# Short f32 products in a recurrence: halves of the TensorE array by turns, and live blocks only

## The chip, the cores and the metric

The kernel runs on one core of one Trainium2 chip, as a single launch. The metric is device time in microseconds (us) of that launch.

## The reference

One step of a diffusion backbone with one trunk layer: a half-step feed-forward (FFN), a token mixer, a second half-step FFN, and a last RMSNorm. 128 context tokens and 1024 latent tokens go through the same weights; width 1024, all in f32. The mixer adds an attention branch and a bidirectional recurrence (HGRN2) of 8 heads with 64 key and 64 value channels. The change is in the recurrence:

```python
b = jnp.cumsum(logf.reshape(B, n, CHUNK, H, DK), axis=2)
diff = b[:, :, :, None] - b[:, :, None, :]
decay = jnp.where(mask, jnp.exp(jnp.where(mask, diff, 0.0)), 0.0)
A = jnp.einsum('bntshk,bnthk,bnshk->bnhts', decay, qc, kc)
o_intra = jnp.einsum('bnhts,bnshv->bnthv', A, vc)
...
def step(S, inp):
    gj, dSj = inp
    return jnp.exp(gj)[..., None] * S + dSj, S
...
o_inter = jnp.einsum('bnthk,bnhkv->bnthv', qc * jnp.exp(b), S_prev)
return (o_intra + o_inter).reshape(B, T, H, DV), s_final
```

For each head the state S decays channel by channel with the forget gate f and takes in the outer product of k = 1 - f and v; the output is S read by q. It is done once forwards and once backwards in time, and the two outputs are added.

## The kernel before

All activations lie transposed: channels on the 128 partitions, the 1152 tokens (1024 latent, 128 context) along the free axis, in three blocks of 384 (`CW`), visited in `ORDER` = 2, 0, 1. The order of phases is FFN 1, mixer (recurrence, then attention), merge and FFN 2. The large products are done on values split into a high and a low float32r part, three matmuls for one (`mm3`, L446 to L448, tiles `mm` in the recurrence). The recurrence's own products are plain f32.

The recurrence (`hgrn`) loops over 8 heads. Partitions 0 to 63 (`A`) hold the head's forward channels, 64 to 127 (`B`) the backward ones. A block of 384 tokens is three tiles of 128 tokens. For each head and block:

- `scan_pre` makes, within groups of 8 tokens, running products of gates (`X`, `Y`), from them decayed keys `Kb` and queries `Qb`, then `KE` and the block's part of `QP` (keys carried to the end of their group, queries from its start), and the group's whole decay `Tm`.
- `scan_lev` builds the 128 x 128 matrix of each tile. First the base products, `Kb` by `Qb` for `A` and for `B` apart (L858, each contracting 64 rows), masked into `A1` and `A2` within groups of 8. Then four decay levels m = 8, 16, 32, 64: `kr[m]` is a copy of `KE` in which only the half-groups that count are not zero, one matmul for a tile with the full 128 rows (L873) gives both directions, and `KE` and `QP` are multiplied by the decay of a neighbour half-group (L884). The outcome goes into `A1` through a mask (L888), at level 64 by two ScalarE copies (L890, L891). Then `Af = A1 + A2`, a transpose of `KE` (L899), and the state increment `dS` (L905).
- After the three blocks `scan_out` runs the states `S` over the eight latent tiles on VectorE (L916) and forms the outputs: for each block and tile a product of `V` with `Af` (L924) and, for latent tiles, of `S` with `QP` (L928), added in one PSUM tile `po`. A head's 64 value channels take one half of the array's columns, rows `r` of `po`; ScalarE copies them to `oT`.

These are generators: between their steps the loop in `hgrn` takes one turn of projection work of the next heads (`work`, 12 matmuls of `mm` in a turn) and one step of the next block's `scan_pre`, and this is the order in which instructions are written; the scheduler of the framework may move them. PSUM has three banks for level and base products (`lv`), three for transposes, increments and outputs (`sm`) and two for projections (`mm`). A PSUM tile is reused when the engine that reads it is done.

Of the kernel before, what the change touches and what calls it, by code (L numbers as in the profile page):

```python
# [9 lines left out]
F32 = mybir.dt.float32  # L10
F32R = mybir.dt.float32r
BF16 = mybir.dt.bfloat16
U8 = mybir.dt.uint8
# [6 lines left out]
P = 128  # L20
# [6 lines left out]
CW = 384  # L27
# [3 lines left out]
ORDER = (2, 0, 1)  # L31
# [56 lines left out]
class Trunk:  # L88
# [514 lines left out]

    def mixer_consts(self, cp):
        nc, a = self.nc, self.a
        self.mask = cp.tile([P, 5, P], U8, name="mask")
        mf = self.tt(F32, "maskf")[:, : 5 * P]
        nc.scalar.dma_start(mf, a["mask"])
        nc.vector.tensor_copy(self.mask.rearrange("p a b -> p (a b)"), mf)
        self.onesb = cp.tile([P, P], F32, name="onesb")  # L610
        nc.vector.memset(self.onesb, 0.0)
        nc.vector.memset(self.onesb[0:64, 0:64], 1.0 / 64)
        nc.vector.memset(self.onesb[64:128, 64:128], 1.0 / 64)
        self.onesq = cp.tile([P, P], F32, name="onesq")
        nc.vector.memset(self.onesq, 1.0 / 384)
        self.onesk = cp.tile([P, P], F32, name="onesk")
        nc.vector.memset(self.onesk, 1.0 / 256)
# [89 lines left out]
    def hgrn(self):  # L707
        nc = self.nc
        self.mmb = 2
        for tag, n in (("lv", 3), ("sm", 3), ("mm", 2)):  # L710
            self.pp.tile([P, 512], F32, tag=tag, bufs=n, name=tag)
        f32 = lambda n, sh: self.fp.tile(sh, F32, name=n)
        A, B = slice(0, 64), slice(64, P)
        self.kr = {m: [f32(f"kr{m}_{i}", [P, CW]) for i in range(1)] for m in (8, 16, 32, 64)}
        self.XY = [f32(n, [P, 48, 8]) for n in "XY"]
        self.A1 = [f32(f"A1_{i}", [P, 3, P]) for i in range(2)]
        self.A2 = [f32("A2", [P, 3, P])]
        for m in self.kr:
            for t in self.kr[m]:
                nc.vector.memset(t, 0.0)  # L720
        for t in self.XY:
            nc.vector.memset(t[:, :, 3:4], 1.0)
        for t in self.A1 + self.A2:
            nc.vector.memset(t, 0.0)
        self.cnt = 0
        heads = [{} for _ in range(H)]
        pairs = [{} for _ in range(4)]
        sgs = [self.proj_sg(j) for j in range(2 * KT)]

        def feed(h):  # L730
            p = h // 2
            r = [self.proj_f(5 * p + h % 2, h, heads[h])]
            if h % 2 == 0:
                r += [self.proj_q(5 * p + 2, pairs[p]), self.proj_v(5 * p + 3, pairs[p])]
            return r

        for i, _ in enumerate(weave(feed(0))):
            if i < 12:
                next(self.tail, None)
            if i == 11:  # L740
                assert next(self.tail, 1)
        def scan_of(h):
            p = h // 2
            if h % 2 == 0:
                pairs[p]["o"] = self.tt(F32, "oT")
            d = heads[h]
            d.update(pairs[p])
            d["h"], d["QP"], d["As"] = h, self.tt(F32, "QP"), {}
            d["Gall"] = self.fp.tile([P, 9], F32, tag="Gall", bufs=2, name="Gall")
            return d  # L750

        def work_of(h):
            p = h // 2
            work = feed(h + 1) if h + 1 < H else []
            if h and h % 2 == 0:
                work = [self.proj_gate(5 * p - 1, p - 1, pairs[p - 1]["o"])] + work
            while len(work) < 4:
                work.append(sgs.pop())
            return chain(*work)

        d = scan_of(0)
        for _ in self.scan_pre(d, ORDER[0]):
            pass
        for h in range(H):
            work = work_of(h)
            for n, b in enumerate(ORDER):
                nd, pre = None, iter(())
                if n < NCH - 1:
                    pre = self.scan_pre(d, ORDER[n + 1])
                elif h + 1 < H:  # L770
                    nd = scan_of(h + 1)
                    pre = self.scan_pre(nd, ORDER[0])
                for _ in self.scan_lev(d, b):
                    next(work, None)
                    next(pre, None)
                for _ in pre:
                    next(work, None)
            for _ in self.scan_out(d):
                next(work, None)
            for _ in work:  # L780
                pass
            oT, d = d["o"], nd
        for _ in self.proj_gate(19, 3, oT):
            pass
# [51 lines left out]
    def scan_lev(self, d, b):  # L836
        nc = self.nc
        V, QP, hh, Gall = d["V"], d["QP"], d["h"] % 2, d["Gall"]
        A, B = slice(0, 64), slice(64, P)
        c0 = b * CW  # L840
        tmp = self.tmp
        if b == ORDER[0]:
            d["dS"] = self.fp.tile([P, 9, 64], F32, tag="dS", bufs=1, name="dS")
            S = d["S"] = self.fp.tile([P, 8, 64], F32, tag="S", bufs=1, name="S")
# [3 lines left out]
        A1, A2 = self.A1[self.cnt % 2], self.A2[0]  # L848
        self.cnt += 1
        Kb, Qb, KE, Tm = d["pre"]  # L850
        bc = lambda t, m: t.unsqueeze(2).to_broadcast([t.shape[0], t.shape[1], m])
        qp = QP[:, c0 : c0 + CW]
        lv = lambda: self.pp.tile([P, 3, P], F32, tag="lv", bufs=3, name="lv")
        mb = lambda i: self.mask[:, i].unsqueeze(1).to_broadcast([P, 3, P])
        for r, dst, mi in ((A, A1, 0), (B, A2, 1)):
            ps = lv()
            for j in range(3):
                nc.tensor.matmul(ps[:, j], Kb[r, ts(j, P)], Qb[r, ts(j, P)], start=True, stop=True)  # L858
            nc.vector.copy_predicated(dst, mb(mi), ps)
        hm = lambda t, m: t.rearrange("p (n h m) -> p n h m", h=2, m=m)  # L860

# [5 lines left out]
        key_half(8)  # L867
        yield
        for li, m in enumerate((8, 16, 32, 64)):
            kr = self.kr[m][0]  # L870
            ps = lv()
            for j in range(3):
                nc.tensor.matmul(ps[:, j], kr[:, ts(j, P)], qp[:, ts(j, P)], start=True, stop=True)  # L873
            tv = Tm.rearrange("p (n h) -> p n h", h=2)
            tL, tR = tv[:, :, 0], tv[:, :, 1]
            Tn = Gall[:, 3 * b : 3 * b + 3] if m == 64 else tmp(f"T{2 * m}", 3, (P, CW // (2 * m)))
            for r, eng, t, side, tt in (
                (A, nc.vector, KE, 0, tR),
                (B, nc.vector, KE, 1, tL),
                (A, nc.gpsimd, qp, 1, tL),  # L880
                (B, nc.vector, qp, 0, tR),
            ):
                v = hm(t, m)[r, :, side]
                eng.tensor_tensor(v, v, bc(tt[r], m), ALU.mult)  # L884
            nc.vector.tensor_mul(Tn, tL, tR)
            if m < 64:
                key_half(2 * m)
                nc.vector.copy_predicated(A1, mb(2 + li), ps)  # L888
            else:
                nc.scalar.copy(A1[A, :, B], ps[A, :, B])  # L890
                nc.scalar.copy(A1[B, :, A], ps[B, :, A])  # L891
            Tm = Tn
            yield
        Af = tmp("Af", 4, (P, 3, P))
# [14 lines left out]
    def scan_out(self, d):  # L909
        nc = self.nc  # L910
        h, V, QP, Gall, S, dS = d["h"], d["V"], d["QP"], d["Gall"], d["S"], d["dS"]
        A, B = slice(0, 64), slice(64, P)
        nc.sync.dma_start(self.o["st"][h], dS[:, 8])
        for j in range(7):
            for r, s0, s1, g in ((A, j, j + 1, j), (B, 7 - j, 6 - j, 7 - j)):
                nc.vector.scalar_tensor_tensor(S[r, s1], S[r, s0], Gall[r, g : g + 1], dS[r, g], ALU.mult, ALU.add)  # L916
        yield
        off = 64 * (h % 2)
        r = slice(off, off + 64)
        for b in ORDER:  # L920
            po = self.pp.tile([P, 3, P], F32, tag="sm", bufs=3, name="po")
            for j in range(3):
                t = 3 * b + j
                nc.tensor.matmul(  # L924
                    po[r, j], V[:, t * P + off : t * P + off + 64], d["As"][b][:, j], start=True, stop=(t == 8)
                )
                if t < 8:
                    nc.tensor.matmul(po[r, j], S[:, t], QP[:, ts(t, P)], start=False, stop=True)  # L928
            nc.scalar.copy(d["o"][r, b * CW : (b + 1) * CW], po[r].rearrange("p a b -> p (a b)"))
            yield  # L930

    def rec_norm(self, c, oT, sq):
# [834 lines left out]
def mask_table():  # L1767
    import numpy as np

    s, t = np.arange(P)[:, None], np.arange(P)[None, :]  # L1770
    same = lambda b: s // b == t // b
    m = [same(8) & (s <= t), same(8) & (s >= t)]
    m += [same(2 * b) & ~same(b) for b in (8, 16, 32)]
    return np.concatenate(m, 1).astype(np.float32)


# [33 lines left out]
```

## Time and profile before

| | |
|---|---|
| median of 3 runs | 2985.35 us (2982.49 to 2985.77) |
| span of the profiled execution, first to last instruction | 2987.2 us |
| busy time in it: PE, VectorE (DVE), ScalarE (ACT), GpSimd (POOL) | 2879.0, 2026.6, 1238.5, 1029.7 us |
| mean granted TensorE clock | 0.987 |
| first and last base product (L858) | 885.7 and 1470.8 us |
| first and last head output product (L924) | 955.4 and 1500.0 us |

No time of the profiled execution beside its span was recorded. PE is TensorE's matmuls, PEld its weight loads, which overlap them. An f32 matmul leaves two records of weight load and matmul in the trace (a transpose one). The time of a PE record includes its way through the array, so records overlap; how fast PE goes is read from start to start. In lists of groups the columns are busy time, mean ns of one, and idle time of the engine just before with what ended it; in lists of waits, the total, the count and the longest one.

### The profile page before, as it was taken

How to read it: one execution, taken by the hardware profiler on the slowest of the kernel's cores; microseconds unless marked ns; L12 is line 12 of the kernel's file. 1: busy time of each engine (PE TensorE's matmuls, PEld its weight loads, DVE VectorE, ACT ScalarE, POOL GpSimd, SP SyncE). 2: the span in 40 equal slices, each digit the busy share in tenths (PEclk: the TensorE clock that was granted, in tenths of full speed). 3: DMA queues.
4: the chain of work that ended last, by engine and by line, in shares of the span. 5: the costliest groups of instructions: out<-in, count | busy, mean ns of one | idle time of the engine just before them, and what ended most of it. 6: DMA issues, size and time to landing. Idle time of an engine off the chain costs nothing. (4 is left out here: it accounts for less than half of the span.)

```text
span 2987.2 us, 49338 instructions
## 1 busy us (share of the span) xinstructions
PE 2879.0 (96%) x18498; PEld 2739.4 (92%) x18498; DVE 2026.6 (68%) x4238; ACT 1238.5 (41%) x2374; POOL 1029.7 (34%) x939
## 2 busy tenths in 40 slices
PE   6999999999989999999998999989999999999998
PEld 5999999999979989898997777779999999999997
DVE  7677777677677777878456677756674665546665
ACT  6432332321364555555244777731462233232112
POOL 0223223453243333323244445532342322226431
PEclk9999999999999999999998999999999999999999
DMA  6643433743121111111110000242352322235211
GB/s 242 205 142 120 133 121 118 265 138 116 63 64 56 38 44 38 54 38 51 60 48 12 16 15 25 62 161 82 123 176 94 106 88 75 74 110 210 91 45 64
DMA packets 151470, 282.37 MB, mean 95 GB/s; under 512 B 19200, under 2 KB 83648, under 8 KB 151232
## 3 DMA queue, kind: packets, MB, share of 16 engines
q1 hardware_dynamic: 151088, 278.90, 28.3%
q8 instruction: 146, 2.39, 0.3%
q14 instruction: 92, 0.75, 0.1%
q10 hardware_dynamic: 144, 0.33, 0.0%
HBM read 215.64 MB, written 63.52 MB: 93 GB/s over the span
## 5 line engine op out<-in xcount | busy, mean ns | idle before, releaser
L1560 PE MATMUL b<-xo,wo 128*128 128x288 f32 x3552 | 484.8, 296 | 0.0
L1560 PEld LDWEIGHTS b<-xo,wo 128*128 128x128 f32 x3552 | 476.6, 188 | 0.0
L475 DVE SCALAR_TENSOR_TENSOR x<-dn,modt,x 128x256 f32<-128x256 f32 (+4 forms) x728 | 353.4, 505 | 169.2 <-PE dn L448 168.1
L235 POOL TENSOR_TENSOR wl<-raw,wh 128x1024 fp32r<-128x1024 f32 (+1 forms) x106 | 235.4, 2222 | 418.7 <-ACT wh L234 353.0
L1560 PE MATMUL b<-bh,wo 128*128 128x288 f32 x1776 | 365.9, 295 | 0.8 <-ACT et L1570 0.8
L446 PE MATMUL mm<-xh,wh 128*128 128x384 f32 (+1 forms) x1008 | 360.5, 358 | 6.1 <-DVE q L665 4.1
L448 PE MATMUL mm<-xh,wl 128*128 128x384 f32 (+1 forms) x1008 | 342.2, 340 | 2.1 <-POOL wl L235 1.9
L447 PE MATMUL mm<-xl,wh 128*128 128x384 f32 (+1 forms) x1008 | 342.0, 339 | 0.0
L1560 PEld LDWEIGHTS b<-bh,wo 128*128 128x128 f32 x1776 | 289.1, 188 | 1.0 <-ACT et L1570 1.0
L1560 PE MATMUL b<-bl,wo 128*128 128x288 f32 x888 | 261.7, 295 | 0.0
L234 ACT CAST wh<-raw 128x1024 fp32r<-128x1024 f32 (+1 forms) x108 | 104.3, 968 | 257.2 <-PE dn L447 165.8
L1535 ACT CAST wo<-raw 128x512 fp32r<-128x512 f32 x185 | 114.7, 621 | 229.0 <-PE b L1560 116.9
L446 PEld LDWEIGHTS mm<-xh,wh 128*128 128x128 f32 (+1 forms) x1008 | 190.2, 189 | 16.0 <-DVE q L665 4.9
L446 PE MATMUL dn<-hh,wh 128*128 128x384 f32 (+2 forms) x576 | 196.3, 341 | 2.0 <-DVE x L475 1.1
L1536 DVE TENSOR_TENSOR wo<-raw,wo 128x512 fp32r<-128x512 f32 x185 | 127.1, 688 | 103.3 <-ACT wo L1535 100.3
L448 PE MATMUL dn<-hh,wl 128*128 128x384 f32 (+2 forms) x576 | 194.7, 338 | 1.0 <-POOL wl L235 1.0
L447 PE MATMUL dn<-hl,wh 128*128 128x384 f32 (+2 forms) x576 | 194.2, 337 | 0.0
L448 PEld LDWEIGHTS mm<-xh,wl 128*128 128x128 f32 (+1 forms) x1008 | 189.7, 188 | 3.6 <-POOL wl L235 2.2
L447 PEld LDWEIGHTS mm<-xl,wh 128*128 128x128 f32 (+1 forms) x1008 | 190.4, 189 | 1.7 <-issue 0.4
L1638 POOL TENSOR_TENSOR hl<-hr,hh 128x1152 fp32r<-128x1152 f32 x44 | 117.9, 2689 | 197.1 <-ACT hh L1637 105.8
L1292 POOL TENSOR_TENSOR ehl<-e,ehl 128x512 fp32r<-128x512 f32 x93 | 122.1, 1318 | 143.8 <-ACT ehl L1290 83.6
L306 DVE SCALAR_TENSOR_TENSOR junk<-wada,cb 128x512 bf16<-128x512 f32 x224 | 165.9, 741 | 5.3 <-DMA wada<-in_w_aT 4.5
(388 smaller groups left out, 7125.0 us busy)
## 6 DMA issues: line engine op xcount, KB each, us to landing
raw<-in_w SPq DMA_DIRECT2D x148, 256.0 KB, 2.9
raw<-in_w SPq DMA_DIRECT2D x58, 512.0 KB, 3.7
wada<-in_w_aT SPq DMA_DIRECT2D x112, 256.0 KB, 2.8
hr<-hs SPq DMA_DIRECT2D x44, 576.0 KB, 5.6
hs<-et SPq DMA_DIRECT2D x148, 144.0 KB, 1.8
raw<-in_w_in SPq DMA_DIRECT2D x41, 512.0 KB, 3.6
hb<-hd SPq DMA_DIRECT2D x44, 288.0 KB, 3.2
x<-in_xT SPq DMA_DIRECT2D x16, 576.0 KB, 6.2
```

Of the source, the lines that this page charges most:

```text
L234: pin(self.nc.scalar.copy(wh, raw))
L235: pin((eng or self.nc.gpsimd).tensor_sub(wl, raw, wh))
L306: nc.vector.scalar_tensor_tensor(junk, ws[n % 2], 1.0, cs[s], ALU.mult, ALU.mult, accum_out=o)
L446: pin(nc.tensor.matmul(ps, wh, xh, start=start and i == 0, stop=False))
L447: pin(nc.tensor.matmul(ps, wh, xl, start=False, stop=False))
L448: pin(nc.tensor.matmul(ps, wl, xh, start=False, stop=stop and i == n - 1))
L475: nc.vector.scalar_tensor_tensor(self.x[m][:, a:b], ps[:, a - lo : b - lo], self.modt[:, gm, m, s : s + 1], self.x[m][:, a:b], ALU.mult, A ...
L1292: eng.tensor_sub(el, e, eh)
L1535: nc.scalar.copy(wh, src[i])
L1536: nc.vector.tensor_sub(wl, src[i], wh)
L1560: nc.tensor.matmul(ps, w[:, k], x[:, k, :QW], start=first, stop=last, skip_group_check=home != i)
L1638: nc.gpsimd.tensor_sub(hl, raw, hh)
```

## The change

Three edits in the recurrence:

1. Base products: the matmuls of the row halves `A` and `B` are written by turns, tile by tile, and both masked copies come after them.
2. Levels 32 and 64: instead of one matmul of a tile with 128 rows and masked result, only the blocks that count are formed. At level 32 there are four for a tile, each with 64 rows, 32 columns of keys and 32 of queries; at level 64 two, of 64 by 64. Forward blocks go into one `lv` bank and backward ones into another. ScalarE copies each kind of block into `A1` (four copies at level 32, two at level 64). Level 64 reads `KE` itself; `kr[64]`, its copies and the mask of level 32 are gone.
3. Head outputs: instead of three groups by block, two groups by distance from the middle of the sequence, tiles (3,4), (2,5) and then (1,6), (0,7), (8). The first of each pair goes to PSUM rows and array columns 0 to 63, the second to 64 to 127. Each group's two halves are copied out apart.

```diff
@@ scan_lev
-        for r, dst, mi in ((A, A1, 0), (B, A2, 1)):
-            ps = lv()
-            for j in range(3):
+        pair = (A, lv()), (B, lv())
+        for j in range(3):
+            for r, ps in pair:
                 nc.tensor.matmul(ps[:, j], Kb[r, ts(j, P)], Qb[r, ts(j, P)], start=True, stop=True)
+        for dst, mi, (_, ps) in zip((A1, A2), (0, 1), pair):
             nc.vector.copy_predicated(dst, mb(mi), ps)
...
         for li, m in enumerate((8, 16, 32, 64)):
-            kr = self.kr[m][0]
-            ps = lv()
-            for j in range(3):
-                nc.tensor.matmul(ps[:, j], kr[:, ts(j, P)], qp[:, ts(j, P)], start=True, stop=True)
+            blocks = []
+            if m < 32:
+                kr, ps = self.kr[m][0], lv()
+                for j in range(3):
+                    nc.tensor.matmul(ps[:, j], kr[:, ts(j, P)], qp[:, ts(j, P)], start=True, stop=True)
+            else:
+                kr, pair = KE if m == 64 else self.kr[m][0], (lv(), lv())
+                blocks = [
+                    (ps, r, slice(k, k + m), slice(q, q + m))
+                    for u in range(0, P, 2 * m)
+                    for ps, r, k, q in ((pair[0], A, u, u + m), (pair[1], B, u + m, u))
+                ]
+                for j in range(3):
+                    kj, qj = kr[:, ts(j, P)], qp[:, ts(j, P)]
+                    for ps, r, k, q in blocks:
+                        nc.tensor.matmul(ps[k, j, :m], kj[r, k], qj[r, q], start=True, stop=True)
...
-            if m < 64:
+            if m < 32:
                 key_half(2 * m)
                 nc.vector.copy_predicated(A1, mb(2 + li), ps)
-            else:
-                nc.scalar.copy(A1[A, :, B], ps[A, :, B])
-                nc.scalar.copy(A1[B, :, A], ps[B, :, A])
+            for ps, _, k, q in blocks:
+                nc.scalar.copy(A1[k, :, q], ps[k, :, :m])
@@ scan_out
-        for b in ORDER:
+        for pairs, lows, highs in (((3, 4), (2, 5)), (2, 4), (4, 6)), (((1, 6), (0, 7), (8,)), (0, 2), (6, 9)):
             po = self.pp.tile([P, 3, P], F32, tag="sm", bufs=3, name="po")
-            for j in range(3):
-                t = 3 * b + j
-                nc.tensor.matmul(
-                    po[r, j], V[:, t * P + off : t * P + off + 64], d["As"][b][:, j], start=True, stop=(t == 8)
-                )
-                if t < 8:
-                    nc.tensor.matmul(po[r, j], S[:, t], QP[:, ts(t, P)], start=False, stop=True)
-            nc.scalar.copy(d["o"][r, b * CW : (b + 1) * CW], po[r].rearrange("p a b -> p (a b)"))
+            at = lambda t: po[A, t - lows[0]] if t < lows[1] else po[B, t - highs[0]]
+            for pair in pairs:
+                for t in pair:
+                    w = V[:, t * P + off : t * P + off + 64]
+                    nc.tensor.matmul(at(t), w, d["As"][t // 3][:, t % 3], start=True, stop=(t == 8))
+                for t in pair:
+                    if t < 8:
+                        nc.tensor.matmul(at(t), S[:, t], QP[:, ts(t, P)], start=False, stop=True)
+            for half, (t0, t1) in ((A, lows), (B, highs)):
+                pv = po[half, : t1 - t0].rearrange("p a b -> p (a b)")
+                nc.scalar.copy(d["o"][r, t0 * P : t1 * P], pv)
             yield
```

The mask table and its tile shrink from five masks to four, and the `kr[64]` buffer goes.

More of the change, by code (lines that the diff above doesn't have):

```diff
@@ L605, in mixer_consts @@
         nc, a = self.nc, self.a
-        self.mask = cp.tile([P, 5, P], U8, name="mask")
-        mf = self.tt(F32, "maskf")[:, : 5 * P]
+        self.mask = cp.tile([P, 4, P], U8, name="mask")
+        mf = self.tt(F32, "maskf")[:, : 4 * P]
         nc.scalar.dma_start(mf, a["mask"])
@@ L713, in hgrn @@
         A, B = slice(0, 64), slice(64, P)
-        self.kr = {m: [f32(f"kr{m}_{i}", [P, CW]) for i in range(1)] for m in (8, 16, 32, 64)}
+        self.kr = {m: [f32(f"kr{m}_{i}", [P, CW]) for i in range(1)] for m in (8, 16, 32)}
         self.XY = [f32(n, [P, 48, 8]) for n in "XY"]
@@ L1772, in mask_table @@
     m = [same(8) & (s <= t), same(8) & (s >= t)]
-    m += [same(2 * b) & ~same(b) for b in (8, 16, 32)]
+    m += [same(2 * b) & ~same(b) for b in (8, 16)]
     return np.concatenate(m, 1).astype(np.float32)
```

## The prediction

> **What bounds the kernel now.** I read the page's first part, then the busy times of the recurrence stage (880 to 1520 us, found by the lines of the changed tiles), then the waits inside it.
>
> ```profile
> span 2987.2 us, 49338 instructions
> PE 2879.0 (96%) x18498; PEld 2739.4 (92%) x18498; DVE 2026.6 (68%) x4238; ACT 1238.5 (41%) x2374; POOL 1029.7 (34%) x939
> 880.00:1520.00 640.00, 610.20 (x3834) 574.58 (x3834) 471.25 (x1026) 332.75 (x686) 200.68 (x232) 0.99 0.15 49
> PE lv L873 <- DVE QP L884: 17.3, 15, 2.3
> PE lv L873 <- POOL QP L884: 4.9, 6, 1.2
> DVE A L859 <- PE lv L858: 68.3, 8, 10.4
> ```
>
> PE is busy 96% of the span and 610.2 of the stage's 640 us, at a granted clock of 0.99; VectorE is busy 471. So in this stage a microsecond taken out of PE's stream is a microsecond off the end, with one exception: of the 30 us in which PE is idle, 22.2 (17.3 + 4.9, 21 waits) lie ahead of a level product, which waits for VectorE or GpSimd to update QP. PE time saved shortly before such a wait is given back in it. At the first base product of each of the eight heads it is the other way round: VectorE waits up to 10.4 us for PE (68.3 us in all), so what is saved at a head's end is kept.
>
> The page's span, 2987.2 us, is 1.85 us above the runs' median of 2985.35; savings read from the trace are taken off the median unscaled.
>
> **What a group of short products costs PE.** Groups of f32 products stand inside the long stream of projection matmuls (mm). I price a group from the start of the last mm before it to the start of the second mm behind it, less the two mm steps that this stretch would take anyway. Six stretches of PE's timeline (start, duration):
>
> ```profile
> 1083.17 0.34 PE L447 MATMUL mm<-xl,wh 128*128 128x384 f32 x1
> 1083.34 0.34 PE L448 MATMUL mm<-xh,wl 128*128 128x384 f32 x1
> 1083.61 1.26 PE L858 MATMUL lv<-Qb,Kb 64*128 64x128 f32 x12
> 1084.80 0.44 PE L446 MATMUL mm<-xh,wh 128*128 128x384 f32 x1
> 1085.08 0.34 PE L447 MATMUL mm<-xl,wh 128*128 128x384 f32 x1
> ...
> 1005.08 0.93 PE L858 MATMUL lv<-Qb,Kb 64*128 64x128 f32 x6
> 1005.94 0.55 PE L678 MATMUL vt<-ident,t 128*128 128x128 f32 x3
> ...
> 1086.83 0.34 PE L448 MATMUL mm<-xh,wl 128*128 128x384 f32 x1
> 1087.02 0.83 PE L873 MATMUL lv<-QP,kr 128*128 128x128 f32 x6
> 1087.60 0.42 PE L446 MATMUL mm<-xh,wh 128*128 128x384 f32 x1
> 1087.86 0.34 PE L447 MATMUL mm<-xl,wh 128*128 128x384 f32 x1
> ...
> 955.09 0.34 PE L448 MATMUL mm<-xh,wl 128*128 128x384 f32 x1
> 955.36 0.43 PE L924 MATMUL po<-Af,V 128*64 128x128 f32 x2
> 955.63 0.38 PE L928 MATMUL po<-QP,S 128*64 128x128 f32 x2
> 955.84 0.38 PE L924 MATMUL po<-Af,V 128*64 128x128 f32 x2
> 956.06 0.38 PE L928 MATMUL po<-QP,S 128*64 128x128 f32 x2
> 956.28 0.38 PE L924 MATMUL po<-Af,V 128*64 128x128 f32 x2
> 956.59 0.44 PE L446 MATMUL mm<-xh,wh 128*128 128x384 f32 x1
> 956.87 0.34 PE L447 MATMUL mm<-xl,wh 128*128 128x384 f32 x1
> ...
> 60.49 1.95 PE L161 MATMUL pb<-modt,raw 128*128 128x2 f32 x16
> 62.30 0.38 PE L448 MATMUL ps<-bh,wl 128*128 128x288 f32 x1
> ...
> 23.82 2.37 PE L251 MATMUL adap<-wada,sc 128*32 128x256 f32 x40
> ```
>
> One mm step is 0.17 us (1083.17 to 1083.34), two are 0.35. Every f32 product leaves two records.
>
> - Level product, whole array: 1086.83 to 1087.86 is 1.03, less 0.35 = 0.68 for 6 records. They take (0.68 - 0.02)/6 = 0.11 each, and the group hardly costs anything at its edges.
> - Base products, half the rows: 1083.34 to 1085.08 is 1.74, less 0.35 = 1.39 for 12 records. Six alone take 0.86 from first start to next start (1005.08 to 1005.94). Twelve one after another would take 0.86 + 6 x 0.11 = 1.52; they took 1.19 (1083.61 to 1084.80), 0.33 less: three records of one half ran beside three of the other. So the two row halves can run together and today do so only where one half's list meets the other's. The 12 records fill 9 slots, and 1.39 - 9 x 0.11 = 0.4 is the price of entering and leaving a split array.
> - Head outputs, half the columns: 955.09 to 956.87 is 1.78, less 0.35 = 1.43 for 10 records. From 955.63 to 956.28 six records take 0.65, 0.11 each, all in one column half, one after another. The edges cost 1.43 - 1.09 = 0.34. A group of 12 is 1.65.
> - The ada product goes through four column quarters by turns: 40 records of 256 columns in 2.37 us, 0.06 each, although 256 columns stream twice as long as 128. Alternate column parts overlap.
>
> **The change, part by part.**
>
> *Base products by turns.* Same 12 records, now A, B, A, B: 6 slots instead of 9. By the row of six alone, 0.27 + 0.86 + 0.28 - 0.35 = 1.06 against 1.39: 0.33 x 24 blocks = 7.9 us less. Of it, what falls ahead of a PE wait in the same block is lost; with 21 waits over 24 blocks I take half: 4 us back. The first copy into A1 now waits for both halves' products, which end together; VectorE has copied one after the other anyway.
>
> *Head outputs.* Per head now 12 + 12 + 10 records in three groups: 1.65 + 1.65 + 1.43 = 4.73. After: two groups, 16 records in 8 slots (t = 3,4,2,5) and 18 in 10 (the last, t = 8, has no partner): 8 x 0.11 + 0.34 = 1.22 and 10 x 0.11 + 0.34 = 1.43, together 2.65. That is 2.08 x 8 heads = 16.6 us less, at heads' ends, where the VectorE wait of up to 10.4 us says it is kept. ScalarE copies four pieces of 256 to 384 columns instead of three of 384; it is idle 307 of the stage's 640 us. One of the four turns of projection work inside this part goes, and is done behind it.
>
> *Levels 32 and 64.* Six records of 128 columns become 24 (level 32: four blocks in four different array parts, 64 rows x 32 columns) and 12 (level 64: two parts of 64 x 64), and both now pay for splitting the array: 0.4 + 6 slots each against 0.68. No row shows so short a record. Price from below: the slot shrinks with the columns, 0.03 and 0.06, since weight loads get shorter with fewer columns:
>
> ```profile
> L873 PEld LDWEIGHTS lv<-QP,kr x576: 186/192/192, 894.3 to 1481.9; 128*128 128x128 f32 x192
> L924 PEld LDWEIGHTS po<-Af,V x144: 132/137/137, 955.4 to 1499.9; 128*64 128x64 f32 x144
> L251 PEld LDWEIGHTS adap<-wada,sc x128: 106/109/110, 23.8 to 58.5; 128*32 128x32 f32 x128
> ```
>
> (192, 137, 109 ns for 128, 64, 32 columns: 0.85 ns a column). Then 0.58 + 0.76 = 1.34 for 1.36, nothing gained (24 x 0.02 = 0.5 us). From above: a slot of 0.11 whatever the columns, as 16 records that stream two columns still take 0.11 each (60.49 to 62.30); then 2 x 1.06 = 2.12, and 24 x 0.76 = 18 us more. That row loads 128 columns of weights, so I stay near the lower end: 0.06 for both, 2 x 0.76 = 1.52, 24 x 0.16 = 4 us more.
>
> By the Trainium skill's "TensorE: Matmul & The Clock Gate", section "Wait - 56ns, not 53.3ns?", starts of matmuls never come closer than about 25 ns however few the columns; 36 records would then take 0.9 us, and by it this part would come to an estimated 8 us more instead of 4. It speaks against blocks this small; the ada row (0.06 a record) does not decide it.
>
> *Other engines at these levels.* VectorE drops the masked copy at level 32 (0.59 us a block), ScalarE the key copy for level 64 (two of 0.35) and takes four copies of 32 partitions instead:
>
> ```profile
> L888 DVE COPY_PREDICATED A<-mask,lv x72: 579/592/605, 898.0 to 1480.0; 128x384 f32<-128x384 uint8 x72
> L891 ACT COPY A<-lv x24: 313/314/316, 906.6 to 1483.2; 64x192 f32<-64x192 f32 x24
> L884 DVE TENSOR_TENSOR KE<-KE,T 64x192 f32<-64x192 f32 x192 | 83.9, 437 | 6.7 <-ACT kr L864 3.3
> ```
>
> Two new waits. First, level 64 reads KE itself, so VectorE's two updates of KE (2 x 0.44) wait for that product, and the block's last QP update and the next block's preparation queue behind them. Who needs KE next is the transpose on PE, a turn of 12 mm (2.1 us) later, which covers 0.9; I cost it at nothing, balanced by the 0.59 saved. Second, each level 32 or 64 takes two of the three lv banks, so level 64's second bank is free only once ScalarE has copied level 32's out: four copies of at most 0.31, 1.2 us, plus ScalarE's queue, again against 2.1 us of mm. I take 3 us for the blocks in which it shows, between 0 and 24 (1 us in every block).
>
> Sum: -7.9 + 4 - 16.6 + 4 + 3 = -13.5 us; 2985.35 - 13.5 = 2971.9, say 2972.
>
> **Rivals.**
>
> *Larger gain.* Nothing given back, levels at the lower price: -7.9 - 16.6 - 0.5 = -25, so 2960. For it: the base saving in a head's first block lies behind VectorE's long wait, and VectorE loses 14 us of masked copies (24 x 0.59). Against: 21 waits at levels.
>
> *The sequencer sets the pace of short records (slower).* If each of the 36 records of levels 32 and 64 needs 0.06 us to issue, as the ada row's mean would allow, they take 2.16 + 0.8 for the edges = 2.96 against 1.36: 24 x 1.6 = 38 us more in place of 4, so 3006. It turns the sign where a record costs over 0.036: 36 x 0.036 + 0.8 = 2.1, 17.5 us more, which eats the other terms (13.5 + 4). Against: a slot of 0.11 for 128 columns runs two records in the base group, so PE issues at 0.055 with ease, and the mm ahead, at 0.17 each, leave the queue time to fill. The same page gives about 62 ns per matmul as the sequencer's price when its hardware decoder is off; by that estimate this rival would hold.
>
> *The new waits show.* Level 64 waits 1 us for ScalarE in every block: 24 instead of 3, so 2993. For it: ScalarE already idles behind PE and runs long casts between. Against: 2.1 us of mm cover.
>
> *The halves do not overlap.* The base group keeps 9 slots and the outputs only lose one group's edges, 0.34 x 8 = 2.7 us: -2.7 + 4 + 3 gives 2990. Against: the overlapped slots of the base group, and the ada row.
>
> **How the numbers follow.** Chances: forecast 0.46, larger gain 0.22, new waits 0.13, sequencer 0.11, no overlap 0.08. 0.2% is 6 us, about what a measurement of this kernel can tell from no change: faster ends below 2979.4. The first two cases give 0.68, and a mild form of the waits 0.02: faster 0.70. Same: waits 0.06, no overlap 0.05: 0.11. Slower (above 2991.3): sequencer 0.11, waits 0.05, no overlap with dearer levels 0.03: 0.19. The range goes from below the larger gain (2960, less the VectorE time that may shorten PE's 22.2 us of waits) to just above the waits case: 2954 to 2994; left out is the sequencer's case and some of the low end.
>
> **What would show it.** Right: 12 base records in about 0.87 us from first start to next mm; head outputs in two groups of 16 and 18 records, about 0.9 and 1.1 us plus edges; levels 32 and 64 in about 0.7 us a group with edges; PE's idle time ahead of levels at 20 to 30 us. Wrong: level groups of over 1.3 us (sequencer), a group of waits of PE at lv for ScalarE's copies of A, or base groups still at 1.19.

## The result: slower by 0.24%

Over 20 runs each, the median went from 2985.02 to 2991.65 us: ratio 1.0024, interval 1.0018 to 1.0030, 6.6 us slower where 13.5 us faster was forecast. The profiled execution's span is 2988.8 us.

The first part of the page after, and the groups of PE in the recurrence stage (880 to 1520 us; busy, mean ns | idle before and what ended it):

```profile
span 2988.8 us, 50507 instructions
PE 2853.6 (95%) x19074; PEld 2701.7 (90%) x19074; DVE 2022.0 (68%) x4213; ACT 1243.1 (42%) x2430; POOL 1030.1 (34%) x939
...
L875 PE MATMUL lv<-QP,kr 128*128 128x128 f32 x288 | 40.4, 277 | 6.5 <-DVE QP L897 6.4
L858 PE MATMUL lv<-Qb,Kb 64*128 64x128 f32 x288 | 24.0, 291 | 0.0
L886 PE MATMUL lv<-QP,KE 64*64 64x64 f32 x288 | 18.3, 227 | 12.5 <-DVE QP L897 11.7 <-POOL QP L897 0.8
L938 PE MATMUL po<-Af,V 128*64 128x128 f32 x144 | 16.3, 284 | 0.0
L911 PE MATMUL kt<-ident,KE 128*128 128x128 f32 x72 | 13.4, 297 | 28.3 <-DVE KE L897 28.3
L941 PE MATMUL po<-QP,S 128*64 128x128 f32 x128 | 12.4, 273 | 0.0
L886 PE MATMUL lv<-QP,kr 64*32 64x32 f32 x576 | 10.8, 196 | 1.4 <-DVE QP L897 1.3
```

The transposes of KE (tile `kt`) in the kernel before, same stage:

```profile
L899 PE MATMUL kt<-ident,KE 128*128 128x128 f32 x72 | 11.7, 271 | 0.0
```

PE has 25 us less to do (2879.0 to 2853.6), as intended, and the end did not move forward. The row to look at is L911, the transposes of KE: 28.3 us of idle time ahead of them, all of it ended by VectorE's update of KE. That wait did not exist before. Stage by its end points, first base product to last output product:

```profile
L858 PE MATMUL lv<-Qb,Kb x288: 271/272/375, 887.7 to 1480.5; 64*128 64x128 f32 x144
L941 PE MATMUL po<-QP,S x128: 272/273/273, 963.8 to 1506.7; 128*64 128x128 f32 x128
```

887.7 to 1506.7 is 619.0 us; before it was 885.7 to 1500.2, 614.5. The stage got 4.5 us longer, which is most of the loss by the medians. The two profiled executions differ by only 1.6 us in span, because what follows the stage took 1482 us in this one and 1487 in the one before.

### The profile page after: what moved, and what is told of

It is laid out like the page before. It is cut to its first block, busy times and chain, and to the rows that moved or that the text cites. A ratio compares the mean times of both kernels' runs of the same rounds, so it can differ in the third digit from the quotient of the medians.

```text
span 2988.8 us, 50507 instructions
## 1 busy us (share of the span) xinstructions
PE 2853.6 (95%) x19074; PEld 2701.7 (90%) x19074; DVE 2022.0 (68%) x4213; ACT 1243.1 (42%) x2430; POOL 1030.1 (34%) x939
```

## What the new groups cost PE

Four stretches of PE's timeline after (start, duration):

```profile
1127.04 0.34 PE L448 MATMUL mm<-xh,wl 128*128 128x384 f32 x1
1127.31 0.94 PE L858 MATMUL lv<-Qb,Kb 64*128 64x128 f32 x12
1128.18 0.44 PE L446 MATMUL mm<-xh,wh 128*128 128x384 f32 x1
1128.46 0.34 PE L447 MATMUL mm<-xl,wh 128*128 128x384 f32 x1
...
1136.02 0.34 PE L448 MATMUL mm<-xh,wl 128*128 128x384 f32 x1
1136.28 0.39 PE L886 MATMUL lv<-QP,kr 64*32 64x32 f32 x24
1136.60 0.44 PE L446 MATMUL mm<-xh,wh 128*128 128x384 f32 x1
1136.88 0.34 PE L447 MATMUL mm<-xl,wh 128*128 128x384 f32 x1
...
1138.63 0.34 PE L448 MATMUL mm<-xh,wl 128*128 128x384 f32 x1
1138.90 0.56 PE L886 MATMUL lv<-QP,KE 64*64 64x64 f32 x12
1139.39 0.44 PE L446 MATMUL mm<-xh,wh 128*128 128x384 f32 x1
1139.67 0.34 PE L447 MATMUL mm<-xl,wh 128*128 128x384 f32 x1
...
1123.50 0.34 PE L448 MATMUL mm<-xh,wl 128*128 128x384 f32 x1
1123.77 0.44 PE L938 MATMUL po<-Af,V 128*64 128x128 f32 x4
...
1125.02 0.44 PE L446 MATMUL mm<-xh,wh 128*128 128x384 f32 x1
1125.30 0.34 PE L447 MATMUL mm<-xl,wh 128*128 128x384 f32 x1
```

Priced as in the prediction (first mm start to second mm start behind, less 0.35 us): base products 1.42 - 0.35 = 1.07 (was 1.39, forecast 1.06); level 32 0.86 - 0.35 = 0.51 (was 0.68, forecast 0.76, lower bound 0.58); level 64 1.04 - 0.35 = 0.69 (was 0.68, forecast 0.76); the output group of 18 1.80 - 0.35 = 1.45 (forecast 1.43). The group of 16, by the median of the eight, is 1.22 (forecast 1.22). So four short blocks run side by side, 24 records in 0.32 us from first start to the next mm, and PE's own bill falls by 6.7 (21 base groups; in three blocks a transpose splits the group before and after) + 16.5 + 4.1 - 0.2 = 27 us.

Against that stand the 28.3 us at kt, about 2 us less waiting ahead of level products (20.2 for 22.2), and the clock. Around one of the long waits (stretch, length, then busy time and count of PE, PEld, DVE, ACT and POOL, granted clock, DMA share, GB/s):

```profile
1108.00:1111.40 3.40, 0.21 (x2) 0.00 (x0) 3.31 (x6) 0.00 (x0) 0.81 (x1) 1.00 0.40 148
1111.40:1112.40 1.00, 0.97 (x5) 0.97 (x6) 0.96 (x4) 0.15 (x1) 0.00 (x0) 0.60 0.05 21
1112.40:1114.90 2.50, 2.50 (x10) 2.50 (x9) 1.91 (x9) 0.32 (x1) 0.00 (x0) 0.50 0.02 7
1114.90:1118.00 3.10, 3.10 (x21) 3.10 (x20) 1.16 (x5) 0.81 (x2) 0.00 (x0) 0.98 0.17 63
```

After 3.2 us without work the granted clock is 0.50 for 3.4 us, and the starts of mm lie 0.32 us apart instead of 0.17. The stage has five such stretches of halved clock, four of them behind waits at kt of 2.9 to 3.2 us; before it had two, one of them behind a wait of 2.35 us. The Trainium skill's "TensorE: Matmul & The Clock Gate", "What's actually happening", describes this: an idle window of about 3.4 us halves the clock, and the windows run freely. The trace agrees on the half, on the 3.4 us and on the free run (all five begin on one grid of 3.41 us), but a whole window of idle time was not needed. The three more stretches cost about 3 x 1.7 = 5 us, an estimate. Sum: -27 + 28.3 - 2 + 5 = +4.3, for 4.5 measured in the stage.

## Why the transposes wait

VectorE and GpSimd in the 8 us around that wait:

```profile
1105.38 0.53 PE L886 MATMUL lv<-QP,KE 64*64 64x64 f32 x10 [0.41 <-DVE QP L897]
1111.43 0.78 PE L911 MATMUL kt<-ident,KE 128*128 128x128 f32 x3 [3.22 <-DVE KE L897]
...
1105.26 1.05 DVE L811 RECIPROCAL Y<-X 128x144 f32<-128x144 f32 x1
1106.23 3.17 DVE L897 TENSOR_TENSOR KE<-KE,T 64x192 f32<-64x192 f32 x2
1109.43 1.35 DVE L813 RECIPROCAL X<-Y 128x192 f32<-128x192 f32 x1
1110.70 0.67 DVE L897 TENSOR_TENSOR KE<-KE,T 64x192 f32<-64x192 f32 x2
...
1106.44 2.36 POOL L235 TENSOR_TENSOR wl<-raw,wh 128x1024 fp32r<-128x1024 f32 x1
```

Level 64's product ends at 1105.91. The update of KE that must follow it, since the product reads KE, runs at 1110.70 to 1111.37, and the transposes start at once. Between lie two updates of the next block's KE and a reciprocal, ahead of it in VectorE's order. One of these updates takes 2.78 us instead of 0.35: it meets GpSimd's wl (the subtraction that makes the low part of projection weights, 1106.44 to 1108.80) and ends just behind it. Over the 24 blocks the update is done 3.3 us on average after the product's end; the 12 mm between give 2.3 us. Before, nothing tied the two: KE's updates waited only for ScalarE's key copies, and counting the 192 updates eight to a block, the last one of each block ended 11 to 30 us *ahead* of the end of that block's level 64 product.

Theory 1: this tie (level 64 reading KE) costs the 28 + 5 us, the rest of the change is a gain. Theory 2: VectorE's chain sets the pace, and PE time saved anywhere comes back in the next wait.

## Experiments

Each run: its median, that of the kernel before on the same chip, and the ratio with its interval.

**e1_own_copy.** 2966.86 for 2987.52: 0.9930 (0.9917 to 0.9942).

```diff
-        self.kr = ... for m in (8, 16, 32)}
+        self.kr = ... for m in (8, 16, 32, 64)}
-                kr, pair = KE if m == 64 else self.kr[m][0], (lv(), lv())
+                kr, pair = self.kr[m][0], (lv(), lv())
...
-            if m < 32:
-                key_half(2 * m)
+            if m < 64:
+                key_half(2 * m)
+            if m < 32:
                 nc.vector.copy_predicated(A1, mb(2 + li), ps)
```

> The changed kernel, but level 64 reads a copy of KE (kr[64], written by ScalarE as in the kernel before) and not KE itself; all other parts of the change stay. Theory 1 (reading KE ties its last update, and so the transposes on PE, behind the level 64 product): PE's waits at kt fall from 28.3 us to under 3, no clock drop behind them, and the saving of about 27 us that the groups' prices give shows: 2957 to 2966 us. Theory 2 (VectorE's chain sets the pace of the recurrence, and PE time saved anywhere comes back in the next wait): the waits at kt go, those ahead of the level products grow from 20 to 35 to 45 us: 2976 to 2986 us.

PE's waits in the stage (total, times, longest):

```profile
PE lv L886 <- DVE QP L897: 12.2, 14, 2.0
PE lv L875 <- DVE QP L897: 8.9, 6, 2.6
PE vt L678 <- ACT t L675: 4.9, 4, 2.4
```

No wait at kt, and those ahead of level products stay at 23 us (with 1.8 for GpSimd): two copies of 0.35 us on ScalarE for each block are worth 27 us. Theory 1, just above its range (the kernel before ran 2.5 us higher here than over the 20 runs). The 27 us of PE work were not all kept; 20.7 were. Most of the rest went to the clock: the time lost to it, estimated as (1 - mean granted clock) x span over all runs, is 41.5 us here (0.9860) and 36.6 in the kernel before on this chip (0.9877). In the trace of e1 the stage has seven stretches of halved clock for two before, behind waits of 2.0 to 2.6 us.

**e2_base_turns, e3_outputs, e4_levels**: each edit of the change alone on the kernel before (the diffs of the change's section, one at a time).

> The kernel before with the base products by turns alone. Theory 1: the group costs 1.07 us instead of 1.39, 7 us less in all, of which up to half comes back ahead of level products: 2977 to 2982 us. Theory 2: all of it comes back: 2983 to 2987 us.

> The kernel before with the new head outputs alone. Theory 1: two groups of 1.22 and 1.45 us for three of 1.66, 1.66 and 1.44, 16.7 us less over eight heads, kept: 2966 to 2971 us. Theory 2: comes back in the next head's waits: 2976 to 2986 us.

> The kernel before with the live blocks of levels 32 and 64 alone (level 64 reads KE itself). Theory 1: products 3.5 us cheaper, 28 us of waits at kt and 3 to 6 us of halved clock more: 3008 to 3018 us. Theory 2: the waits are there only because PE arrives early through the other two parts; alone the levels cost little: 2984 to 2995 us.

| | median, before | ratio |
|---|---|---|
| e2, base products by turns | 2984.11, 2987.52 | 0.9987 (0.9978 to 0.9996) |
| e3, outputs | 2975.07, 2987.52 | 0.9963 (0.9951 to 0.9975) |
| e4, levels, level 64 reading KE | 3009.63, 2987.52 | 1.0074 (1.0061 to 1.0086) |

-3.4, -12.4 and +22.1 us add up to +6.3, the whole change's loss. e4 shows the same wait without the other two edits, so it does not come from PE's arriving early; theory 2 said under 10 us here.

```profile
PE kt L910 <- DVE KE L896: 28.5, 19, 3.2
```

e2 keeps half of its 6.7 us (by the interval, 1.2 to 6.6). Its time of 2984.1 lies in theory 2's range; by the ratio, on the 2985.02 of the 20 runs, it would be 2981, in theory 1's. The half that is missing did not come back ahead of level products, where PE waits as long as before:

```profile
PE lv L874 <- DVE QP L885: 18.7, 18, 2.6
PE lv L874 <- POOL QP L885: 3.4, 3, 1.8
```

That is 22.1 us for 22.2, and the mean clock of the runs is the same (0.988), so where it went stays open. e3 lies between both ranges and gave 4 us less than the price says; its waits ahead of level products grew to 26.8 us from 22.2. So only e3 shows what theory 2 says, and in part.

**e10_levels_copy**: e4 with the own copy of e1. 2980.63 for 2986.14: 0.9980 (0.9971 to 0.9989).

> The kernel before with the live blocks of levels 32 and 64, level 64 on its own copy of KE; base products and outputs as before. Theory 1: without the tie the levels keep their price, 3.5 us less than whole-array products, part of it given back: 2979 to 2985 us, no waits at kt (with the tie and nothing else changed it was 1.0074). Theory 2 (short blocks cost by themselves, in banks or ScalarE copies, not only by the tie): 2988 to 2998 us.

The blocks by themselves are a gain of 5.5 us, no wait at kt is left, and the tie alone makes them a loss of 22.

**e5_later_transposes.** 2978.61 for 2986.46: 0.9974 (0.9964 to 0.9984).

```diff
             Tm = Tn
             yield
+        yield
         Af = tmp("Af", 4, (P, 3, P))
```

> The changed kernel with one more turn of 12 mm between level 64 and the transposes of KE, 4.2 us of cover instead of 2.1. Theory 1 (KE's last update is done 3.3 us on average after level 64's product, 5.5 at most, whatever PE does meanwhile): the waits at kt fall from 28.3 to under 6 us, no clock drop behind them: 2962 to 2972 us. Theory 2 (PE only waits for a VectorE that is late anyway, and would wait as long later): waits ahead of the level products take over, 2982 to 2992 us.

```profile
PE lv L886 <- DVE QP L897: 19.9, 17, 2.3
PE mm L446 <- DVE q L665: 8.4, 4, 2.3
PE kt L912 <- DVE KE L897: 1.3, 3, 0.8
```

With 24 mm of cover the wait at kt goes, as theory 1 says, but the time lies between both ranges, and only 15 of the 33 us come back (1.0024 to 0.9974): 27.3 us ahead of level products instead of 20.2, and 8.4 ahead of mm. The clock took more too, by the same estimate 46.5 us for 39.9 in the changed kernel: none of its drops lies behind a wait at kt any more, but behind the other waits the stage has ten stretches of halved clock for five. The place of all that follows was moved too, so this run proves the length of the cover and not the price of the tie.

**e6_wl_pieces.** 3002.73 for 2986.46: 1.0054 (1.0042 to 1.0067).

```diff
+        if self.mode == "mix" and eng is None and shape[1] == KT:
+            for v in range(4):
+                k = slice(2 * v, 2 * v + 2)
+                pin(self.nc.gpsimd.tensor_sub(wl[:, k], raw[:, k], wh[:, k]))
+            return wh, wl
         pin((eng or self.nc.gpsimd).tensor_sub(wl, raw, wh))
```

> The changed kernel with GpSimd's subtraction for the mixer's w_in weights (wl, 2.4 us for one) written in four pieces of 0.6 us. Theory 1a (a short VectorE operation that meets wl is held until it ends: in the changed kernel one of 2.7 to 2.9 us instead of 0.2 to 0.4 lies between level 64 and KE's update in 8 of 24 blocks, with 19 of the 28 us of waits): held for at most 0.8 us, waits at kt 12 to 18 us, clock drops gone: 2972 to 2983 us. Theory 1b (the update is late because of its place in VectorE's order alone, and the long ones are chance): waits at kt stay at 25 to 30 us, 2988 to 2995 us.

```profile
1105.43 2.79 POOL L238 TENSOR_TENSOR wl<-raw,wh 128x256 fp32r<-128x256 f32 x4
...
1105.22 3.60 DVE L902 TENSOR_TENSOR KE<-KE,T 64x192 f32<-64x192 f32 x2
```

A miss: the time lies above both ranges, and pieces did not help where it counts. In the eight blocks where a VectorE operation between level 64 and KE's update had begun 0.2 to 0.45 us before the first piece, it was held past the last one's end, as the first of the two updates here for 3.2 us, longer than with one piece (2.78). Elsewhere VectorE did get in between the pieces: the update of Kb that took 1.92 us beside the one wl of the changed kernel (1129.25) took 0.95 beside four pieces (1129.73), and from 880 to 1520 us the VectorE operations of over 1.5 us fell from 31 to those 8. So the edit left the very holds in place that it was to shorten, and the waits at kt, still 28.6 us, do not tell 1a from 1b; that the eight grew with wl's length speaks for 1a. The added 9 us go with the clock: by the same estimate it took 53.4 us for 39.9.

**e9_wl_vector.** 2965.28 for 2986.14: 0.9934 (0.9920 to 0.9948).

```diff
+        if self.mode == "mix" and shape[1] == KT:
+            eng = self.nc.vector
         pin((eng or self.nc.gpsimd).tensor_sub(wl, raw, wh))
```

> The changed kernel with the subtraction wl for the mixer's projection weights on VectorE and not on GpSimd. In the changed kernel and in the one with four pieces every VectorE operation of over 2 us runs beside a wl and ends 0.02 to 0.4 us after it. Theory 1a (VectorE is held by wl, and that is what makes KE's last update late in 8 blocks): no VectorE operation between level 64 and KE's update over 1.5 us; VectorE takes about 36 x 1.2 = 43 us of new work; waits at kt 10 to 18 us instead of 28, time 2975 to 2990 us. Theory 1b (the place in VectorE's order alone): VectorE's new work lies in the same places, waits at kt 25 us or more, 2990 to 3005 us.

```profile
PE kt L913 <- DVE KE L899: 14.4, 13, 1.5
...
L237 DVE TENSOR_TENSOR wl<-raw,wh 128x1024 fp32r<-128x1024 f32 (+1 forms) x36 | 43.6, 1212 | 77.1 <-ACT wh L234 76.7
```

The tie is still there, VectorE has 43.6 us of new work, and yet the waits at kt halve, none is over 1.5 us, and the loss of 6.6 us becomes a gain of 21. The time is 10 us below 1a's range, the waits are inside it. This decides for 1a: about half of the wait came from VectorE being held by GpSimd, the other half (14.4 us) from the update's place behind other work.

**e11_copy_vector** (e1 and e9 together): 2960.50 for 2986.82, 0.9915 (0.9901 to 0.9928). **e12_before_vector** (e9's edit on the kernel before): 2976.90 for 2986.82, 0.9971 (0.9960 to 0.9982).

> Both cures on the changed kernel: level 64 on its own copy of KE, and wl on VectorE. Theory 1 (the waits at kt are the tie times a late VectorE): each cure alone gave 0.993; the tie's remaining 14 us of waits at kt go too: 2948 to 2958 us. Theory 2 (both remove the same thing): 2962 to 2968 us.

> The kernel before with wl on VectorE and nothing else. Theory 1: there are no waits at kt in it, KE runs ahead of the products, and PE's waits ahead of level products (22 us) may shrink: 2970 to 2984 us, less gained than the changed kernel gained by the same edit (26 us). Theory 2 (wl on VectorE is worth the same in any version): 2958 to 2964 us.

e11 is the fastest of all and lies between both ranges: the waits at kt are gone, but those ahead of level products are 22.1 us again (15.7 in e9). e12 holds theory 1's range: the same edit is worth 9.9 us without the tie and 27 with it.

**e7_whole_64 and e8_turns_outputs.** 2972.63 for 2986.46: 0.9951 (0.9938 to 0.9965); 2968.95 for 2986.46: 0.9943 (0.9931 to 0.9956).

```diff
 # e7, on e1
-            if m < 32:
+            if m != 32:
                 kr, ps = self.kr[m][0], lv()
...
                 nc.scalar.copy(A1[k, :, q], ps[k, :, :m])
+            if m == 64:
+                nc.scalar.copy(A1[A, :, B], ps[A, :, B])
+                nc.scalar.copy(A1[B, :, A], ps[B, :, A])
```

e8 is the kernel before with the base products and the outputs of the change.

> Turns, new outputs and the blocks of level 32; level 64 as before, whole-array product on its own copy. Level 64 in blocks costs 0.69 us a group, as much as the whole-array one at 0.68, so by price nothing changes against the kernel with blocks of level 64 and an own copy (ratio 0.993): 2964 to 2970 us. If the banks of lv mattered (level 64 takes one instead of two), 3 us less than that.

> Turns and new outputs on the kernel before, all levels as before. Theory 1: the parts add (3.4 and 12.4 us were measured apart): 2969 to 2973 us, and the blocks of level 32 are worth 3 to 5 us on top. Theory 2: VectorE's chain leaves no more than the outputs' share: 2973 to 2977 us.

e8 adds up (3.4 + 12.4 = 15.8 from e2 and e3, 17.5 measured). e7 is a miss: blocks of level 32 without those of level 64 gained nothing over e8, although their price is 4 us less. PE waits 29.9 us ahead of level products in e7, 20.9 in e8, 22.9 in e1, and the clock's estimated cost is 44.6 us in e7 for 39.2 in e8. Why the chain falls that way was not settled; the order that the framework's scheduler gives to VectorE differs in all three.

## Why the prediction was wrong

The time, 2991.65 us, lies inside the stated range, but the kernel got slower where faster was forecast. Without the tie (e1) it gained 20.7 us, between the forecast (13.5) and the rival "larger gain" (25).

- *Base products, outputs*: prices of 1.06, 1.22 and 1.43 us forecast; 1.07, 1.22 and 1.45 measured. "Half given back" came out in size for the base products in e2 (3.4 of 6.7 kept), but by luck: the waits ahead of level products, in which it was to be lost, did not grow. "Kept" was too much for the outputs: e3 kept 12.4 of 16.5. No term of the sum stood for the clock.
- *Levels 32 and 64 on PE*: dearer by 4 us was forecast, 4 us cheaper came. The lower bound, a slot in proportion to the columns, was the right end, and even high (0.51 for 0.58). The sequencer rival is refuted: 24 records in 0.32 us are 0.013 each, below the 0.036 at which the sign would turn, and below the 25 ns between starts that the prediction cites from the Trainium skill's "TensorE: Matmul & The Clock Gate", section "Wait — 56ns, not 53.3ns?"; the trace differs, so 25 ns does not hold across parts of a split array.
- *The failed step* is "First, level 64 reads KE itself ... which covers 0.9; I cost it at nothing". It measured 28.3 us of waits and an estimated 5 of halved clock, and taking the tie away brought 27 us back. The cover was right, 2.3 us. The time to be covered was wrong: 0.9 us is the update's own length, but an update that can only be issued when the product is done stands in VectorE's order behind what was placed ahead of it, and any of that may be held by GpSimd for 2.4 us; 3.3 us is what it took. Nor did the step see that in the kernel before KE's updates ran 11 to 30 us ahead, so that the edit did not shorten a margin but removed one.
- *The rival "the new waits show"* had about the right time (2993) by luck, since another wait is its mechanism. Of its own, level 64 for ScalarE's copies of level 32, the trace after shows at most three cases, 6.9 us at the weight loads; the matmuls at the same places are put down to VectorE's QP, so which of the two ended those waits is open.

## What to carry to other kernels

A copy that looks like waste can be what lets a chain on another engine run ahead: before reading the original, look in the trace how far ahead of the reader the next writer is today. And the cover of a new wait is to be set against the whole queue of the engine that ends it, held operations included, not against the length of the one operation that is waited for. Where a saving does not show in full, read the granted clock before calling it given back: in e1, e5 and e6 the clock took 5 to 14 us more than in the kernel that each is compared with.

## What the runs showed of the hardware

- Parts of the array in rows and columns (64 x 32, four at a time) take 24 f32 records in 0.32 us; a group of base or output products in a split array costs 0.34 to 0.41 us at its edges (1.22 - 8 x 0.11, 1.07 - 6 x 0.11), so it pays only where it saves more.
- Every VectorE operation from 880 to 1520 us that took over 1.5 us ran beside a GpSimd wl and ended 0.02 to 0.42 us after it (25 of 25 before, 31 of 31 after). The Trainium skill's "SBUF — State Buffer", "SBUF: two separate sides", calls this an exclusive lock on a shared port pair, held for a whole instruction by whichever engine starts first; the lengths agree. But in 8 of the 31 the profile, whose times on GpSimd are rough, has the VectorE operation start first, by 0.2 to 0.45 us, and it was held all the same, so these start times alone do not tell which engine is held. In e6 these eight were held past four GpSimd instructions in a row, 3.2 to 3.3 us, while elsewhere VectorE got in between the four and no operation took over 1.5 us. In e9, moving the 36 wl to VectorE (43.6 us of work) left VectorE less busy: 436.1 us of the 600 from 880 to 1480, for 449.4 in the changed kernel.
